# LayerNorm's scale and shift of the plain x and its residual addition as one VectorE step in the second MLP segment

## The chip, the cores and the metric

The kernel runs on one core of one Trainium2 chip (trn2), in one launch. The metric is the device time of that launch in microseconds. A difference of about 0.2% (3.3 us here) is what a measurement of this kernel can tell from no change.

## The reference, cut to what matters

Two encoder layers over 512 tokens of 1024 channels, all in float32. In each layer a token sublayer (attention, retention, gates) gives `y`, and then:

```python
def layer_norm(x, g, b):
    mu = jnp.mean(xf, axis=-1, keepdims=True)
    var = jnp.mean(jnp.square(xf - mu), axis=-1, keepdims=True)
    y = (xf - mu) * lax.rsqrt(var + LN_EPS) * g + b
...
    x = layer_norm(DEEPNORM_ALPHA * x + y, ln1_g[i], ln1_b[i])
    ffn = conv_glu_ffn(x, w_up[i], conv_w[i], conv_b[i], w_down[i])
    ple = jax.nn.sigmoid(x @ w_ple_gate[i]) * (p[i] @ w_ple_proj[i])
    x = layer_norm(DEEPNORM_ALPHA * x + ffn + ple, ln2_g[i], ln2_b[i])
```

The change touches the term `DEEPNORM_ALPHA * x` of the last line: where the normalised x gets its factor and shift, and where it is added to the sum.

## The kernel before, in words

**Matrix products.** float32 operands are split in two float32r parts, `hi` (a cast on ScalarE) and `lo` (the remainder, a subtraction on VectorE), and each product is three matmuls (`hi*hi`, `hi*lo`, `lo*hi`). Weights come as 128x1024 pieces from `in_wpack`. Many products are done in Strassen's manner, with seven instead of eight block products (`a c t1 t2 d t3 t4`), for which sums of weight blocks are made by transfers that add: a POOL-queue transfer adds a second block to `rawa` or `rawt`. In the same way `s`, `sh`, `sl` are sums of blocks of the activations and their two parts.

**Stages of a layer's second half.** `project()` makes x before the norm in four tiles `xn[0..3]` (128 tokens x 1024), and `normed` subtracts the mean and multiplies by 1/std there. `done1` turns `xn` by TensorE into `x1t`, the transposed operand, and applies the norm's factor g and shift b there per partition. `xn` itself, the plain x, is needed once more, for the residual, and gets its g and b (both times ALPHA, which ScalarE puts in on loading: tiles `lnh`) in `affine(t)`: for each half of 512 columns a multiplication and an addition on VectorE, `xn<-xn,lnh`, 16 instructions for the four tiles.

Then comes `pg()`, which runs the list `PG[l]`: the gate product of the embedding (`a c t1 t2 d t3 t4`), with the first of three MLP segments woven in (`0a` to `1t4` and `g`: blocks of the up-projection; `S`: sums; `T2`: second half of `done1`; `A0` to `A3`: `affine`). Then `down(0)`, `up_part(1)`, `down(1)`, `up_part(2)`, and the last down-projection. `R[0..3]` are four tiles that start as the embedding's projection; `ple_gate` multiplies them by the sigmoid of the gate (`R<-R,psg`), x is added, and each segment's down-projection adds its products out of PSUM (`into`: `R<-R,u`, `R<-R,v`).

**Adding x to R.** `RES_DMA = (0, 1)`: for tiles 0 and 1, once both halves of the gate are multiplied in, `residual()` issues a transfer on the POOL queue that adds `xn[t]` to `R[t]` (`R<-xn`, 512 KB). For tiles 2 and 3 `ple_gate` does it on VectorE, a half at a time (`R<-R,xn`).

**Buffers.** `xn`, `R`, the operands of the down-projection (`a`, `k`, `ss`, `sh`, `sl`), `gg`, `uh`, and part of the `hi`, `lo` and `raw` tiles all come out of one pool, `unit`, of 30 buffers of 128x1024 float32 (`N_UNIT = 30`). A buffer is reused once its last reader has finished. `lnh` has a pool of its own, with four buffers.

**Order.** TensorE's order is that of the program text. From the middle of each layer's first product to the end of `region()` the order on the other four engines, and which buffer a tile takes, is set when the kernel is built, by a planner (`_jobs`, `_dues`, `_best`, `_order`): it gives each instruction a due time from the TensorE work that needs it, walks through the engines with priced instructions and limited buffers, and keeps the best of 120 rounds of a random search started from `SEED`. An instruction under `prog.lazy = prog.pin = True`, as in `affine`, is due no later than the TensorE work that it stands behind in the text. On the chip every engine runs its instructions in that order, and waits for each one's inputs and buffer.

All instructions are issued through one helper, so the profile shows them under one line (L270); tiles tell them apart.

Of the kernel before, what the change touches and what calls it, by code (L numbers as in the profile page):

```python
# [12 lines left out]
ALU = mybir.AluOpType  # L13
# [43 lines left out]

TABLES_AT = ('0t4', '1t4')

PG = (tuple('a 0a T2 c S g S S S g 0c 1a A0 t1 A1 t2 A2 0t1 A3 1c 0t2 0d 0t3 1t1 0t4 d g 1t2 1d 1t3 t3 1t4 g t4'.split()),  # L60
        tuple('a 0a T2 S c S 0c 1a g g S 1c A0 t1 A1 0t1 A2 S 0t2 A3 t2 0d 0t3 1t1 0t4 1t2 1d 1t3 d 1t4 g t3 g t4'.split()))
PG_EARLY = "a"
RES_DMA = (0, 1)
A_DEEP = (4, 5, 5)
BOUND = ("p0", "t4a", "tr", "t4b", "p1")
VG_DEEP = 3
VG_PLAN = ("ga2", "0a")
VG_EARLY = "d"
S_SEQ = ("t1", "d", "t2", "t3")
UP_ORDER = ((tuple('0a 0t1 0c g g 0t2 0d 1a 0t3 g 0t4 g 1t1 1c 1t2 1d 1t3 s 1t4 s s s'.split()), tuple('0a 0t1 0c g g 0t2 0d 0t3 g 0t4 1a 1t1 1c 1t2 1d 1t3 s g s 1t4 s s'.split())),  # L70
            (tuple('0a 0t1 0c g g 0t2 0d 1a 0t3 g 0t4 g 1t1 1c 1t2 1d 1t3 s 1t4 s s s'.split()), tuple('0a 0t1 0c g g 0t2 0d 0t3 g 0t4 1a 1t1 1c 1t2 1d 1t3 s g s 1t4 s s'.split())))

DOWN = ("a", "c", "t1", "t2", "d", "t3", "t4")
CAP = {"unit.u": 30, "xt.xt": 1, "raw.raw": 3, "wsplit.hi": 3, "wsplit.lo": 3, "tmp.t": 6, "conv.cw": 2, "bias.B": 4, "psum.b": 8}
# [7 lines left out]
SET = {1: dict(soon=5, hold=6, reserve=10, load=16, work=25, scale=1.0, spare=2, near=10, seed=0, shake=0.0), 2: dict(soon=5, hold=6, reserve=10, load=16, work=25, scale=1.0, spare=2, near=10, seed=0, shake=0.0)}  # L82
ROUNDS = 120
WALK = 12
SEED = 3


VG_HELD = (('0t1', '1t1', '0t2', '0c', '1t2', '1a', '1d', '1t3'), ('0a', '0c', '0t1', '1t1', '1t3', '1t2', '0t3', '0t2', '1d'))
# [2 lines left out]
def _up_order(l, s):  # L91

    return UP_ORDER[l][s - 1] if s else PG[l]


def _up_blocks(l, s):

    t0 = 2 * sum(SEGS[:s])
    return [t0 + 2 * b for b in range(sum(k[0].isdigit() and k.endswith("t4") for k in _up_order(l, s)))]
# [386 lines left out]
def _best(jobs, rounds=None):  # L486

    import random
    rnd = random.Random(SEED)
    rounds = rounds or ROUNDS  # L490
# [289 lines left out]
def trunk(tc, wpack, x_nat, x_tr, head, p_tr, rpb, decay, ln_par, ln_col, conv, cos_t, sin_t, dist, xi_d, zd, ident_d, out):  # L780
    prog = Program(tc)
    nc = _Engines(prog)
# [3 lines left out]
    with ExitStack() as es:  # L786
# [22 lines left out]
        def unit_f(s, shape=(P, 1024)):  # L809
            return up.tile(list(shape), F32, tag="u", name=nm(s))  # L810

        def tmp(s, n=512):
            return tp.tile([P, n], F32, tag="t", name=nm(s))
# [480 lines left out]
        for i in range(2):  # L1294
            c = slice(i * 512, (i + 1) * 512)
# [114 lines left out]
        for l in range(DEPTH):  # L1410
# [380 lines left out]
            xn, xgb = [], []  # L1791
# [223 lines left out]
            def affine(t):  # L2015

                prog.lazy = prog.pin = True
                for h in range(2):
                    z = xn[t][:, h * 512:(h + 1) * 512]
                    nc.vector.tensor_mul(z, z, g1[h])  # L2020
                    nc.vector.tensor_add(z, z, b1[h])
                prog.lazy = prog.pin = False

            def project():
# [81 lines left out]
            R = [unit_f("R") for _ in range(4)]  # L2106
# [35 lines left out]
            def ple_gate(t, c, src, scale):  # L2142
                sg = tmp("psg")
                nc.scalar.activation(sg, src, AF.Sigmoid, scale=scale)
                nc.vector.tensor_mul(R[t][:, c], R[t][:, c], sg)
                if t not in RES_DMA:
                    nc.vector.tensor_add(R[t][:, c], R[t][:, c], xn[t][:, c])
                    return
                done[t] = done.get(t, 0) + 1
                if done[t] == 2:  # L2150
                    late.append(t)

            done, late = {}, []

            def residual():

                while late:
                    t = late.pop(0)
                    nc.gpsimd.dma_start(R[t], xn[t], accum_op=ALU.add)

            wx = {}

# [92 lines left out]
            def up_part(s):  # L2255

                t, state, st, n, S = 2 * sum(SEGS[:s]), {}, {}, 0, {}
                nb = len(_up_blocks(l, s))
                for k in _up_order(l, s):
                    if k in "gs":  # L2260
                        j = 2 * nb + n // 2
                        n += 1
                        up_half(j, t + j, state)
                    else:
                        b = int(k[0])
                        block(b, k[1:], t + 2 * b, st.setdefault(b, {}), None, S)
# [40 lines left out]
            def pg():  # L2307
                S, sg = {}, vg_sums(xf_at(xf))
                two = lambda name: [bank(name) for _ in range(2)]
                keep, u, v, state, blocks, n = {}, None, None, {}, {}, 0  # L2310
                nb = len(_up_blocks(l, 0))
                for key in PG[l]:
                    residual()
                    if key[0] in "TA":
                        (done1 if key[0] == "T" else affine)(int(key[1]))
                        continue
                    if key == "S":
                        r = next(sg)
                        if isinstance(r, dict):
                            S.update(r)  # L2320
                        continue
                    if key == "g":
                        j = 2 * nb + n // 2
                        n += 1
                        up_half(j, j, state)
                        continue
                    if key[0].isdigit():
                        b = int(key[0])
                        block(b, key[1:], 2 * b, blocks.setdefault(b, {}), xt, S)
                        continue  # L2330
                    def product(ps, first):
                        lh = {"a": lambda k, s, i: xt[:, k, s, i * P:(i + 1) * P],
                              "c": lambda k, s, i: xt[:, 4 + k, s, i * P:(i + 1) * P],
                              "t4": lambda k, s, i: xt[:, 4 + k, s, 256 + i * P:256 + (i + 1) * P]}.get(key)
                        if lh is None:
                            lh = lambda k, s, i: S[key][s][:, k, i * P:(i + 1) * P]
                        for j in range(2):
                            hi, lo = ws.get()
                            for i in range(2):
                                for kk in range(2):  # L2340
                                    k, r = 2 * j + kk, slice(kk * 512, (kk + 1) * 512)
                                    mm3(ps[i], lh(k, 0, i), lh(k, 1, i), hi[:, r], lo[:, r], first and k == 0, k == 3, not first)

                    if key in S_SEQ:
                        sums_out(key, S)
                    if key == "a":
                        u = two("u")
                        product(u, True)
                        keep["p1"] = [tmp("p1") for _ in range(2)]
                        for i in range(2):  # L2350
                            nc.scalar.copy(keep["p1"][i], u[i])
                    elif key == "c":
                        w = two("w")
                        product(w, True)
                        for i, t in enumerate(keep["p1"]):
                            nc.vector.tensor_add(t, t, w[i])
                        for i, t in enumerate(keep["p1"]):
                            ple_gate(i, N1, t, 1.0)
                    elif key == "t1":
                        v = two("v")  # L2360
                        product(v, True)
                        p5 = unit_f("p5", (P, 2, 512))
                        for i in range(2):
                            nc.scalar.copy(p5[:, i], v[i])
                    elif key == "t2":
                        product(u, False)
                        keep["u2"] = [tmp("u2") for _ in range(2)]
                        for i in range(2):
                            nc.scalar.copy(keep["u2"][i], u[i])
                    elif key == "d":  # L2370
                        product(v, False)
                        for i, t in enumerate(keep["u2"]):
                            nc.vector.tensor_add(t, t, v[i])
                        for i, t in enumerate(keep["u2"]):
                            ple_gate(i, N2, t, -1.0)
                    elif key == "t3":
                        product(u, False)
                        for i in range(2):
                            nc.vector.tensor_add(p5[:, i], p5[:, i], u[i])
                        for i in range(2):  # L2380
                            ple_gate(2 + i, N2, p5[:, i], -1.0)
                    else:
                        product(u, False)
                        for i in range(2):
                            ple_gate(2 + i, N1, u[i], 1.0)

            pg()
            st = [sp.tile([P, 2, 6], F32, tag="bn", name=nm("bn")) for _ in range(4)]
            residual()
            two = lambda name: [bank(name) for _ in range(2)]  # L2390
            def region():

# [12 lines left out]
            for s in (len(SEGS) - 1,):  # L2405
# [180 lines left out]
                t4 = products("t4", x4, s == 0)  # L2586
# [160 lines left out]
```

## Time and profile before

| | |
|---|---|
| median of 3 runs | 1650.58 us (1649.71 to 1650.64) |
| profiled execution, its own time | 1654.58 us |
| its span from first to last instruction | 1652.8 us |
| TensorE matmuls busy | 1632.7 us, 99% of the span |
| VectorE busy | 1331.4 us, 81% |
| ScalarE busy | 1011.9 us, 61% |
| mean granted TensorE clock | 0.995 |
| `pg()` and `down(0)` of layer 0 | about 447 to 585 us of the span |
| `pg()` and `down(0)` of layer 1 | about 1267 to 1400 us |
| `up_part(1)` of layer 1 | 1400 to 1484 us |

The span is what the trace shows; 1.78 us of the profiled execution lie around it. The profiled execution is 4.0 us above the median of the runs. Times in rows are microseconds from the span's start unless marked ns. In a row of the timeline the bracket gives the engine's idle time before the instruction and what ended it. TensorE's idle time and the stretches in which its clock was granted at half are the two things that can be won here without taking work away from it.

### The profile page before, as it was taken

Reading aid. Unit: us, or ns where it says so; the run is one execution under the profiler, and the core shown is the slowest. Engines: PE = TensorE matmul, PEld = TensorE weight load, DVE = VectorE, ACT = ScalarE, POOL = GpSimd, SP = SyncE. Lnnn points to the kernel's source line nnn. Section 1 sums busy time; section 2 is a strip of 40 time slices with the busy share of each in tenths; the row PEclk is TensorE's granted clock in tenths of the full one; section 3 lists DMA queues with packets and bytes.
Section 4 is the critical chain, followed back from the end, with each engine's and each line's share of the span. In section 5 each row is a group of like instructions: output and inputs, shape, how many; then the busy total and the mean of one; then the engine's idle time right before and its main releaser. Section 6 shows DMA issues by size and latency. Waiting matters only on the chain. (4 is left out here: it accounts for less than half of the span.)

```text
span 1652.8 us, 25767 instructions
## 1 busy us (share of the span) xinstructions
PE 1632.7 (99%) x9717; PEld 1454.2 (88%) x9717; DVE 1331.4 (81%) x2057; ACT 1011.9 (61%) x1522; POOL 267.4 (16%) x320
## 2 busy tenths in 40 slices
PE   9999999999999999999999999999999999999997
PEld 7889999888888898898888899998888987988986
DVE  6657998689997968768885779986799889687688
ACT  6656769654667656456484558795457574563554
POOL 1210212001211121111012112210012111111113
PEclk9999999999999999999999999999999999999999
DMA  8996768969899799888599867787588997988874
GB/s 306 270 244 148 181 154 201 283 204 251 194 296 260 193 257 223 230 259 208 171 263 252 254 166 189 192 227 242 196 252 223 317 238 203 250 198 264 236 178 116
DMA packets 111852, 371.53 MB, mean 225 GB/s; under 512 B 13168, under 2 KB 15728, under 8 KB 111728
## 3 DMA queue, kind: packets, MB, share of 16 engines
q0 software_dynamic: 39888, 143.15, 44.4%
q1 hardware_dynamic: 71840, 226.74, 38.3%
q8 instruction: 76, 1.25, 0.3%
q14 instruction: 48, 0.39, 0.1%
HBM read 336.28 MB, written 27.79 MB: 220 GB/s over the span
## 5 line engine op out<-in xcount | busy, mean ns | idle before, releaser
L270 DVE TENSOR_TENSOR lo<-rawa,hi 128x1024 fp32r<-128x1024 f32 (+1 forms) x214 | 255.9, 1202 | 74.2 <-ACT hi L270 66.9
L270 POOL DMA_DIRECT2D rawa<-in_wpack x162 | 143.4, 905 | 969.5 <-DVE lo L270 681.5
L270 ACT CAST hi<-rawa 128x1024 fp32r<-128x1024 f32 (+1 forms) x214 | 218.8, 1033 | 104.9 <-DMA rawa<-in_wpack 64.2
L270 DVE TENSOR_TENSOR lo<-raw,hi 128x1024 fp32r<-128x1024 f32 (+1 forms) x175 | 211.0, 1209 | 21.4 <-ACT hi L270 18.4
L270 PE MATMUL gt<-x1t,hi 128*128 128x512 f32 x640 | 197.5, 390 | 0.0
L270 ACT CAST hi<-raw 128x1024 fp32r<-128x1024 f32 (+1 forms) x151 | 156.4, 1039 | 38.6 <-PE u L270 17.1
L270 PEld LDWEIGHTS gt<-x1t,hi 128*128 128x128 f32 x640 | 118.8, 188 | 23.6
L270 PE MATMUL gt<-x1t,lo 128*128 128x512 f32 x320 | 124.5, 389 | 0.0
L270 PE MATMUL v<-lo,sh 128*128 128x512 f32 x216 | 84.2, 390 | 0.0
L270 PE MATMUL v<-hi,sh 128*128 128x512 f32 x216 | 84.1, 389 | 0.0
L270 PE MATMUL v<-hi,sl 128*128 128x512 f32 x216 | 84.0, 389 | 0.0
L270 PE MATMUL u<-sh,hi 128*128 128x256 f32 x288 | 81.9, 285 | 0.0
L270 PE MATMUL v<-sh,hi 128*128 128x256 f32 x288 | 81.7, 284 | 0.0
L270 PE MATMUL u<-xt,hi 128*128 128x256 f32 x448 | 81.5, 283 | 0.0
L270 PE MATMUL v<-sh,lo 128*128 128x256 f32 x288 | 81.5, 283 | 0.0
L270 PE MATMUL v<-sl,hi 128*128 128x256 f32 x288 | 81.5, 283 | 0.0
L270 PE MATMUL u<-sh,lo 128*128 128x256 f32 x288 | 81.5, 283 | 0.0
L270 PE MATMUL u<-sl,hi 128*128 128x256 f32 x288 | 81.5, 283 | 0.0
L270 ACT ACTIVATE uh<-u 128x512 f32<-128x512 f32 x60 | 35.8, 596 | 74.4 <-PE u L270 70.3
L270 PE MATMUL u<-hi,sl 128*128 128x512 f32 x200 | 78.7, 394 | 2.6 <-DVE sl L270 2.6
L270 PE MATMUL u<-lo,sh 128*128 128x512 f32 x200 | 78.5, 393 | 1.2 <-DVE lo L270 1.2
L270 PE MATMUL gt<-ybt,hi 128*128 128x512 f32 x256 | 79.5, 392 | 0.0
(310 smaller groups left out, 4791.4 us busy)
## 6 DMA issues: line engine op xcount, KB each, us to landing
raw<-in_wpack SPq DMA_DIRECT2D x171, 512.0 KB, 7.7
rawa<-in_wpack POOLq DMA_DIRECT2D x156, 512.0 KB, 7.4
rawa<-in_wpack SPq DMA_DIRECT2D x52, 512.0 KB, 7.0
rawt<-in_wpack SPq DMA_DIRECT2D x52, 512.0 KB, 7.2
rawt<-in_wpack POOLq DMA_DIRECT2D x52, 512.0 KB, 9.6
hi<-in_wpack POOLq DMA_DIRECT2D x40, 512.0 KB, 7.3
sx<-s_scr SPq DMA_DIRECT2D x32, 512.0 KB, 10.5
lo<-in_wpack POOLq DMA_DIRECT2D x16, 512.0 KB, 8.3
```

The costliest lines, as they stand in the source:

```text
L270: r = o.call(*[real(x) for x in o.a], **{k: real(v) for k, v in o.k.items()})
```

## The change

`affine(t)` gets a third instruction for each half: it adds the finished half of `xn[t]` to `R[t]` on VectorE. Its four calls leave `PG` for the list of the second MLP segment, `up_part(1)`, behind that segment's first two block products. The transfers `R<-xn` and the additions in `ple_gate` are removed, for all four tiles. The planner's search starts from another seed. TensorE's instructions and their order stay as they are; the planned order of the other engines is searched anew.

```diff
-PG = (tuple('a 0a T2 c S g S S S g 0c 1a A0 t1 A1 t2 A2 0t1 A3 1c 0t2 0d 0t3 1t1 0t4 d g 1t2 1d 1t3 t3 1t4 g t4'.split()),
-        tuple('a 0a T2 S c S 0c 1a g g S 1c A0 t1 A1 0t1 A2 S 0t2 A3 t2 0d 0t3 1t1 0t4 1t2 1d 1t3 d 1t4 g t3 g t4'.split()))
+PG = (tuple('a 0a T2 c S g S S S g 0c 1a t1 t2 0t1 1c 0t2 0d 0t3 1t1 0t4 d g 1t2 1d 1t3 t3 1t4 g t4'.split()),
+        tuple('a 0a T2 S c S 0c 1a g g S 1c t1 0t1 S 0t2 t2 0d 0t3 1t1 0t4 1t2 1d 1t3 d 1t4 g t3 g t4'.split()))
-RES_DMA = (0, 1)
 UP_ORDER: the second segment's list, in both layers
-  '0a 0t1 0c g g 0t2 0d 1a 0t3 g 0t4 g 1t1 1c 1t2 1d 1t3 s 1t4 s s s'
+  '0a 0t1 A0 0c A1 g A2 g A3 0t2 0d 1a 0t3 g 0t4 g 1t1 1c 1t2 1d 1t3 s 1t4 s s s'
-SEED = 3
+SEED = 1
 def affine(t):
     prog.lazy = prog.pin = True
     for h in range(2):
-        z = xn[t][:, h * 512:(h + 1) * 512]
+        c = slice(h * 512, (h + 1) * 512)
+        z = xn[t][:, c]
         nc.vector.tensor_mul(z, z, g1[h])
         nc.vector.tensor_add(z, z, b1[h])
+        nc.vector.tensor_add(R[t][:, c], R[t][:, c], z)
     prog.lazy = prog.pin = False
 def ple_gate(t, c, src, scale):
     nc.vector.tensor_mul(R[t][:, c], R[t][:, c], sg)
-    if t not in RES_DMA:
-        nc.vector.tensor_add(R[t][:, c], R[t][:, c], xn[t][:, c])
-        return
-    done[t] = done.get(t, 0) + 1
-    if done[t] == 2:
-        late.append(t)
-done, late = {}, []
-def residual():
-    while late:
-        t = late.pop(0)
-        nc.gpsimd.dma_start(R[t], xn[t], accum_op=ALU.add)
 def up_part(s):
     for k in _up_order(l, s):
-        if k in "gs":
+        if k[0] == "A":
+            affine(int(k[1]))
+        elif k in "gs":
 ...
 def pg():
     for key in PG[l]:
-        residual()
 ...
 pg()
-residual()
```

More of the change, by code (lines that the diff above doesn't have):

```diff
@@ L69 @@
 S_SEQ = ("t1", "d", "t2", "t3")
-UP_ORDER = ((tuple('0a 0t1 0c g g 0t2 0d 1a 0t3 g 0t4 g 1t1 1c 1t2 1d 1t3 s 1t4 s s s'.split()), tuple('0a 0t1 0c g g 0t2 0d 0t3 g 0t4 1a 1t1 1c 1t2 1d 1t3 s g s 1t4 s s'.split())),
-            (tuple('0a 0t1 0c g g 0t2 0d 1a 0t3 g 0t4 g 1t1 1c 1t2 1d 1t3 s 1t4 s s s'.split()), tuple('0a 0t1 0c g g 0t2 0d 0t3 g 0t4 1a 1t1 1c 1t2 1d 1t3 s g s 1t4 s s'.split())))
+UP_ORDER = ((tuple('0a 0t1 A0 0c A1 g A2 g A3 0t2 0d 1a 0t3 g 0t4 g 1t1 1c 1t2 1d 1t3 s 1t4 s s s'.split()), tuple('0a 0t1 0c g g 0t2 0d 0t3 g 0t4 1a 1t1 1c 1t2 1d 1t3 s g s 1t4 s s'.split())),
+            (tuple('0a 0t1 A0 0c A1 g A2 g A3 0t2 0d 1a 0t3 g 0t4 g 1t1 1c 1t2 1d 1t3 s 1t4 s s s'.split()), tuple('0a 0t1 0c g g 0t2 0d 0t3 g 0t4 1a 1t1 1c 1t2 1d 1t3 s g s 1t4 s s'.split())))
 DOWN = ("a", "c", "t1", "t2", "d", "t3", "t4")
```

## The prediction

> **What bounds the kernel now.** I read the page's head first, then TensorE's waits, then its timeline where it waits, then the timeline of the engine waited for, and last the chain.
>
> ```profile
> span 1652.8 us, 25767 instructions
> PE 1632.7 (99%) x9717; PEld 1454.2 (88%) x9717; DVE 1331.4 (81%) x2057; ACT 1011.9 (61%) x1522; POOL 267.4 (16%) x320
> ```
>
> TensorE's matmuls (PE) are busy for 99% of the span of 1652.8 us, and the change takes no matmul away. So all that can be won is TensorE's idle time and what its clock loses. Its waits, all of them that the view lists (waiting engine and tile, releaser: us, times, longest):
>
> ```profile
> PE u L270 <- DVE sl L270: 2.6, 1, 2.6
> PE w L270 <- DVE lo L270: 2.1, 1, 2.1
> PE w L270 <- ACT hi L270: 1.8, 1, 1.8
> PE u L270 <- DVE lo L270: 1.2, 1, 1.2
> PE warm L270 <- DVE warm L270: 1.2, 1, 1.2
> PE st L270 <- ACT kz L270: 0.7, 1, 0.7
> PE s L270 <- DVE qk L270: 0.6, 1, 0.6
> PE kz L270 <- DVE kf L270: 0.5, 1, 0.5
> PE u L270 <- DVE x1t L270: 0.4, 1, 0.4
> PE tr L270 <- DVE xn L270: 0.2, 1, 0.2
> ```
>
> Each of them occurs once. The first four are the largest; the timeline tells when they happen, and the windows view tells what the granted clock was after the largest:
>
> ```profile
> 482.43 0.50 PE L270 MATMUL u<-hi,sl 128*128 128x512 f32 x1 [2.59 <-DVE sl L270]
> 533.23 0.50 PE L270 MATMUL u<-lo,sh 128*128 128x512 f32 x1 [1.24 <-DVE lo L270]
> 1370.98 0.49 PE L270 MATMUL w<-hi,k 128*128 128x512 f32 x1 [1.82 <-ACT hi L270]
> 1373.59 0.80 PE L270 MATMUL w<-lo,k 128*128 128x512 f32 x1 [2.11 <-DVE lo L270]
> ```
>
> ```profile
> 483.91:487.32 3.41, 3.41 (x9) 2.67 (x8) 3.41 (x7) 0.00 (x0) 0.00 (x0) 0.50 1.04 233
> 1373.59:1378.20 4.61, 4.61 (x11) 3.64 (x12) 4.61 (x8) 4.24 (x5) 0.00 (x0) 0.50 0.60 125
> ```
>
> All four lie in the embedding's gate product and first MLP segment, where the change works: two in layer 0, two in layer 1. In a row of the windows the third number from the right, behind the five engines, is the clock: 0.50 for 3.41 us right after the gap of 2.59, and 0.50 for the 4.61 us after the last gap. At half clock half of that time is lost: 1.7 and 2.3 us. So this stage loses 2.59 + 1.24 + 1.82 + 2.11 = 7.76 us idle and 4.0 us by the clock, 11.8 us in all.
>
> Why VectorE was late each time:
>
> ```profile
> 477.00 0.69 DVE L270 TENSOR_TENSOR xn<-xn,lnh 128x512 f32<-128x512 f32 x1
> ...
> 478.74 1.29 DVE L270 TENSOR_TENSOR xn<-xn,lnh 128x512 f32<-128x512 f32 x2
> ...
> 481.08 0.69 DVE L270 TENSOR_TENSOR xn<-xn,lnh 128x512 f32<-128x512 f32 x1
> 481.68 1.29 DVE L270 TENSOR_TENSOR sl<-s,sh 128x512 fp32r<-128x512 f32 x2
> ...
> 530.14 0.76 DVE L270 TENSOR_TENSOR ss<-gg 128x256 f32<-128x256 f32 x2 [1.64 <-DMA R<-xn]
> ...
> 1354.92 0.75 DVE L270 SCALAR_TENSOR_TENSOR gg<-uh,cw,gg 128x511 f32<-128x511 f32 x1
> 1360.75 1.23 DVE L270 TENSOR_TENSOR lo<-rawa,hi 128x1024 fp32r<-128x1024 f32 x1 [5.08 <-DMA R<-xn]
> ```
>
> In layer 0 TensorE waits for `sl` at 481.68, and four instructions of `affine` stand just ahead of it. Later VectorE itself stands still for 1.64 us (layer 0) and 5.08 us (layer 1) until a transfer `R<-xn` has landed. Neither `ss<-gg` nor `lo<-rawa,hi` reads or writes R or xn. What ties them to the transfer is the pool: they are given the buffer that `xn` leaves, and that is free only when the transfer has read it. The chain of waits says the same for the program's end; its longest piece that isn't TensorE is
>
> ```profile
> 1349.67 10.95 DMA R<-xn
> ```
>
> **The change part by part.**
>
> *`affine` leaves this stage.* Its instructions, and the additions that stand there now:
>
> ```profile
> L270 DVE TENSOR_TENSOR xn<-xn,lnh x32: 681/696/711, 461.7 to 1308.6; 128x512 f32<-128x512 f32 x32
> L270 DVE TENSOR_TENSOR R<-R,xn x8: 683/689/699, 563.4 to 1395.5; 128x512 f32<-128x512 f32 x8
> L270 POOL DMA_DIRECT2D R<-xn x4: 867/867/874, 520.3 to 1349.7; - x4
>   DVE R L270: 13.6, 4
> ```
>
> Two of them in a row start 0.60 us apart (478.74 for 1.29 us holds two), so a layer's 16 take 9.6 us of VectorE out of this stage. Four ran just before `sl`: 4 x 0.60 = 2.4 us. Without them the gap of 2.59 us shrinks to 0.2, like the least in the list, and with it goes its half clock: -2.4 - 1.7 = -4.1.
>
> The *transfers go.* Then no buffer waits for them. Behind VectorE's 5.08 us lie the last two gaps (3.93 us) with their half clock (2.3), behind its 1.64 us the gap of 1.24: -7.5. POOL loses four issues of 0.87 us, and 13.6 us in which its queue stood until R was multiplied, with weight additions behind it. I cost that at nothing, since no row of TensorE's waits names a transfer; it can only help.
>
> *24 instructions enter the second segment* in each layer (16, the four additions of tiles 2 and 3, four new ones for tiles 0 and 1): 24 x 0.60 = 14.4 us of VectorE, beside
>
> ```profile
> 1400.30:1431.30 31.00, 31.00 (x217) 29.11 (x216) 15.87 (x17) 13.57 (x17) 5.48 (x7) 1.00 0.98 289
> ...
> 1458.00:1484.20 26.20, 26.20 (x134) 22.41 (x133) 25.29 (x43) 16.83 (x26) 5.30 (x7) 1.00 0.85 183
> sum 167.90, PE 167.90 PEld 151.66 DVE 123.06 ACT 99.30 POOL 31.04; mean PE 27.98 PEld 25.28 DVE 20.51 ACT 16.55 POOL 5.17
> ```
>
> The last row sums six windows that cover this segment in both layers (585 to 669 and 1400.3 to 1484.2): VectorE is idle for 167.90 - 123.06 = 44.8 us, and 28.8 come in. In layer 1 the first 31 us alone have 15.1 idle for 14.4. So I take 0. If the cover is gone, because they slide to the last window (0.9 us idle), up to 13.5 us of VectorE work stand ahead of that segment's operands; that end belongs to the slower side.
>
> *Loads of the constants* (`lnh`, four per layer on SP's queue, and four ScalarE scalings) can come later, into a stage with less traffic; they have a pool of their own: 0.
>
> *The new wait.* Each third instruction waits for the last product that the first segment adds to R:
>
> ```profile
> L270 DVE TENSOR_TENSOR R<-R,u x8: 680/683/700, 1376.2 to 1397.8; 128x512 f32<-128x512 f32 x8
> ```
>
> That is done by 1398.5, ahead of the segment's start at 1400, so the VectorE queue behind it (the segment's convolutions) isn't held. But until then all four `xn` keep their buffers: tiles 0 and 1, which now go by 1360.6 (1349.67 + 10.95), about 38 us longer. These are 2 of 30 buffers, in the very stretch where two instructions waited for such a buffer. The trace has no row for what will be short instead. Its bounds: below, a gain, since the order is searched anew and small gaps elsewhere in it (0.7 + 0.6 + 0.5 + 0.4 + 0.2 = 2.4 us) could close too; above, that the three gaps which hang on a buffer come back in full, 7.5 us. I take one gap of the middle size seen here with one window of half clock, 1.82 + 1.7 = 3.5, as nearest to what a shortage did in this stage.
>
> [...] Both stretches of half clock follow gaps of 1.8 to 2.6 us, so I let them go with the gaps. [...]
>
> Sum: -4.1 - 7.5 + 3.5 = -8.1 us. The profiled execution has 1654.58 (span 1652.8 and 1.78 around it), so 1646.5 for it; the median of the runs is 4.0 lower, and I let both fall by the same: 1650.58 - 8.1 = **1642.5**. If the profile's extra 4.0 us sit in just these waits, the gain in the timed runs is up to 4.0 smaller, 1646.5; without a new gap it is 1639.0. That is the likeliest case's own range.
>
> **The rivals.**
> 1. *Nothing takes the waits' place*: -4.1 - 7.5 = -11.6, 1639.0. For it: VectorE gets 9.6 us back in this stage. Against it: every planned stretch of this trace has some small gap.
> [...]
> 3. *Another buffer wait takes the transfers' place* with the same price in both layers: only `affine`'s share is won, -4.1, less small new gaps of up to 2.4 in the newly searched order: 1646.5 to 1648.9, about no change. For it: `ss` and `lo` waited for exactly such a buffer, and the change frees these later.
> 4. *Slower: a weight block's buffer comes free too late, so that its transfer is issued late and nothing covers it.* Price from the nearest rows: 10.95 us for such a transfer to land plus 1.23 for `lo`, and two windows of half clock, 3.4: 15.6 us for one. With the rest won, -11.6 + 15.6 = +4.0: 1654.6; it decides from new stalls of over 11.6 us upward, and is slower by more than 0.2% (3.3 us, about what can be told from no change) from 14.9. For it: 38 us more of two buffers. Against it: TensorE waited for no transfer in 1652 us.
>
> **How the numbers follow.** Chances: the forecast 0.48, rival 1 0.15, rival 2 0.05, rival 3 0.20, rival 4 0.12. The first three are faster, and a tenth of rival 3: 0.70; the rest of rival 3 is the same: 0.18; rival 4 slower: 0.12. The range reaches from 1637.5 (rival 1 and half of the small gaps closed) to 1653 (rival 3 and most of the way to rival 4), and leaves out about one in ten above and less below.
>
> **What would show it.** In the changed kernel's trace: no `R<-xn`; VectorE has no idle time ended by it; 16 `R<-R,xn` and 32 `xn<-xn,lnh`, all in or near the second segment; TensorE's waits on `sl` and on `lo` or `hi` in these stages gone, and no half clock there. [...] The prediction as a whole is wrong if the gaps in the newly searched order sum to more than the 11.6 us that go.

## The result, and the profile after

| | before | changed |
|---|---|---|
| median of 6 runs | 1652.29 us (1649.71 to 1655.04) | 1644.72 us (1644.16 to 1645.20) |
| ratio, 95% interval | | 0.9953 [0.9940, 0.9966] |
| profiled execution, its span | 1654.58 us, 1652.8 | 1644.46 us, 1642.7 |

The change makes the kernel 0.47% faster, 7.8 us [5.6, 9.9]. Forecast were 8.1 us and a median of 1642.5, which the measured one exceeds by 2.2. The page's head and all of TensorE's waits in the changed kernel (waiting engine and tile, releaser: us, times, longest):

```profile
span 1642.7 us, 25774 instructions
PE 1629.1 (99%) x9717; PEld 1451.7 (88%) x9717; DVE 1336.0 (81%) x2065; ACT 1017.4 (62%) x1525; POOL 267.4 (16%) x316
```

```profile
PE gt L269 <- DVE uh L269: 1.3, 1, 1.3
PE warm L269 <- DVE warm L269: 1.2, 1, 1.2
PE st L269 <- DVE kz L269: 0.5, 2, 0.4
PE o L269 <- DVE ta L269: 0.5, 1, 0.5
PE s L269 <- DVE qk L269: 0.3, 1, 0.3
PE tr L269 <- DVE xn L269: 0.3, 1, 0.3
PE w L269 <- DVE ta L269: 0.3, 1, 0.3
PE gt L269 <- DVE lo L269: 0.2, 1, 0.2
```

They sum to 4.6 us, the list of before to 11.3. All four of the large gaps are gone, and one of 1.3 us is new. The windows view, where before had half clock and over the two gate-product stages (third number from the right: the granted clock):

```profile
1371.37:1378.20 6.83, 6.83 (x32) 5.66 (x31) 6.83 (x10) 3.29 (x7) 1.73 (x2) 1.00 0.58 121
470.00:585.00 115.00, 114.79 (x675) 101.94 (x674) 97.40 (x135) 73.65 (x95) 16.60 (x19) 1.00 0.87 242
1266.00:1400.00 134.00, 133.70 (x781) 118.53 (x780) 119.56 (x165) 88.93 (x123) 21.33 (x25) 1.00 0.92 258
```

The clock is full throughout (1.00 in each row). 6.7 us less of waits and 4.0 us of half clock (half of 3.41 + 4.61 us at 0.50) make 10.7; the span of the profiled executions fell by 10.1. So the gain is where the prediction looked for it. The new gap stands where the moved instructions went (timelines of TensorE and VectorE, layer 0):

```profile
587.73 0.70 PE L269 MATMUL gt<-x1t,hi 128*128 128x512 f32 x2 [1.35 <-DVE uh L269]
```

```profile
580.96 2.49 DVE L269 TENSOR_TENSOR xn<-xn,lnh 128x512 f32<-128x512 f32 x4
583.36 1.28 DVE L269 TENSOR_TENSOR R<-R,xn 128x512 f32<-128x512 f32 x2
584.57 1.29 DVE L269 TENSOR_TENSOR xn<-xn,lnh 128x512 f32<-128x512 f32 x2
585.77 1.22 DVE L269 TENSOR_TENSOR lo<-raw,hi 128x1024 fp32r<-128x1024 f32 x1
586.91 0.68 DVE L269 TENSOR_TENSOR uh<-uh,w 128x512 f32<-128x512 f32 x1
```

Eight instructions of `affine` and a `lo` run ahead of the addition that reads TensorE's product `w` out of PSUM, and TensorE waits 1.35 us for that addition.

### The profile page after: what moved, and what is told of

The parts are those of the page before. It is cut to its first block, busy times and chain, and to the rows that moved or that the text cites. A ratio compares the mean times of both kernels' runs of the same rounds, so it can differ in the third digit from the quotient of the medians.

```text
span 1642.7 us, 25774 instructions
## 1 busy us (share of the span) xinstructions
PE 1629.1 (99%) x9717; PEld 1451.7 (88%) x9717; DVE 1336.0 (81%) x2065; ACT 1017.4 (62%) x1525; POOL 267.4 (16%) x316
## 5 line engine op out<-in xcount | busy, mean ns | idle before, releaser
L269 PE MATMUL u<-hi,sh 128*128 128x512 f32 x200 | 77.8, 389 | 0.0
```

The lines of the kernel that those rows point to most:

```text
L269: r = o.call(*[real(x) for x in o.a], **{k: real(v) for k, v in o.k.items()})
```

## The experiments

The first four ask which part carries the gain. My theory was that `affine` and the transfers did, by leaving the stage; the rival, that it was the order, searched anew.

**Only the seed, on the old kernel.**

```diff
-SEED = 3
+SEED = 1
```

> The kernel before with only the planner's seed changed from 3 to 1; nothing of the change itself. My theory (the gain is the affine instructions and the adding transfers leaving this stage): both stay, so the losses stay in kind: VectorE idle time ended by R<-xn is there again, and the time is within 4 us of the kernel before. Rival (the gain is the newly searched order): the time is 5 to 8 us below before, like the changed kernel.

Measured: 0.9947 [0.9935, 0.9960], 1644.75 us, 8.8 us below before and as fast as the changed kernel. My theory falls; the rival's mechanism came, with a little more than its 5 to 8 us. The transfers are still waited for, but by ScalarE (its waits), and TensorE's longest wait apart from the program's first stage (`warm`) is 0.8 us (its waits, the five largest):

```profile
ACT a L270 <- DMA R<-xn: 1.7, 1, 1.7
ACT hi L270 <- DMA R<-xn: 0.6, 1, 0.6
```

```profile
PE warm L270 <- DVE warm L270: 1.2, 1, 1.2
PE v L270 <- DVE sl L270: 1.2, 2, 0.8
PE s L270 <- DVE qk L270: 0.8, 2, 0.6
PE gt L270 <- DVE x1t L270: 0.8, 1, 0.8
PE v L270 <- DVE R L270: 0.3, 1, 0.3
```

**The change without its seed.**

```diff
-SEED = 1
+SEED = 3
```

> The changed kernel with the planner's seed left at 3. My theory: 5 to 10 us below before, no half clock in the two gate-product stages, no VectorE idle time ended by a transfer of x; against the changed kernel within 3 us. Rival (order): no gain that can be told, within 3 us of before.

Measured: 0.9955 [0.9942, 0.9967], 1645.91 us. That is 7.4 us below before, as my theory said, but it doesn't speak for that theory alone: the changed program's order was searched anew, from the same seed. So the structure without the seed also gives the whole gain. The two don't add: either one suffices.

**Transfers replaced in place, `affine` left where it was.**

```diff
 def residual():
-    nc.gpsimd.dma_start(R[t], xn[t], accum_op=ALU.add)
+    for c in (N1, N2):
+        nc.vector.tensor_add(R[t][:, c], R[t][:, c], xn[t][:, c])
```

> The kernel before with its two transfers R<-xn per layer replaced by VectorE additions at the same place of the text (four more VectorE instructions per layer in the gate-product stage); affine stays where it was, seed 3. My theory: the transfers' share of the gain comes alone, about 7.5 us less 0 to 2.4 for the added VectorE work where it is full: 4 to 7.5 us below before, and a wait on sl or lo behind affine's instructions remains. Rival (VectorE's load in this stage is what counts, not the transfers): no gain or up to 3 us slower, since the stage gets 2.4 us more of VectorE per layer. Rival (order): anything within 4 us of before.

Measured: 0.9960 [0.9947, 0.9974], 1646.43 us. 6.6 us fit my theory's range; the rival of VectorE's load is out, as the stage got 2.4 us per layer more of it and still won. But the theory's sign did not come: `affine` stayed, and yet TensorE's longest wait on `sl` is 0.7 us, where before had 2.6. The order was searched anew here too, and the third reading fits that better.

**The transfer kept for two tiles, in the second segment.**

```diff
 def affine(t):
     for h in range(2):
-        nc.vector.tensor_add(R[t][:, c], R[t][:, c], z)
+        if t > 1:
+            nc.vector.tensor_add(R[t][:, c], R[t][:, c], z)
+    if t < 2:
+        nc.gpsimd.dma_start(R[t], xn[t], accum_op=ALU.add)
```

> The changed kernel, but tiles 0 and 1 of x are added by the transfer again, now behind affine in the second segment; tiles 2 and 3 on VectorE as in the changed kernel; seed 1. My theory (a transfer costs where a short buffer waits for its end): affine's share stays won, at least 4.1 us below before; if VectorE or another engine shows idle time ended by R<-xn in the second segment, up to 5 us of the changed kernel's gain are lost, and if no buffer is short there, the time is that of the changed kernel or up to 1.5 us less, since VectorE has four additions less where the changed kernel has its gap of 1.35 us. Rival (the transfer costs by its traffic, wherever it runs): the weight loads beside it land later and TensorE waits on them.

Measured: 0.9972 [0.9960, 0.9983], 1647.90 us: some 3 us of the changed kernel's gain are missing. No compute engine is idle until an `R<-xn`, so no buffer wait explains it, and my theory, which then allowed for no loss, missed. TensorE's longest waits are on `lo`, `sl` and `hi`. The longest of all, 1.55 us on `sl`, ends at 557.33 us, before the first of these transfers is issued at 570.52; so another order has at least a part in the loss. How much the traffic does is not settled.

**One order held fixed.** To part the terms from the search, the next three play back the order and choice of pools that the planner had found for the kernel before, and edit one thing in it. Their edits are given partly in words.

*The transfers release `xn`'s buffers* (they add another tile, from HBM, so the sum of tiles 0 and 1 lacks x):

```diff
-        order = _best(jobs)
+        order = held order of the kernel before
-    nc.gpsimd.dma_start(R[t], xn[t], accum_op=ALU.add)
+    nc.gpsimd.dma_start(R[t], rscr[l][t * P:(t + 1) * P, :], accum_op=ALU.add)
```

> The kernel before with its planned order and its choice of pools held fixed, instruction for instruction; only the four transfers onto R read the embedding's projection in HBM (r_scr) instead of xn, so x is left out of tiles 0 and 1 and another tile added. They issue at the same place and move the same 512 KB, but no longer hold xn's buffers. Theory (ss and lo waited for the buffer that the transfer was still reading): both VectorE waits of 1.64 and 5.08 us on R<-xn go without another wait in their place, TensorE's gaps of 1.24, 1.82 and 2.11 us and layer 1's half clock with them: 5 to 7.5 us below before. Rival (the transfer's traffic or its share of the POOL queue made the weights late): VectorE still waits there, no more than 2 us of gain.

Measured: 0.9959 [0.9947, 0.9972], 6.8 us [4.6, 8.8] of 1652.69. The buffer is the cause: transfers of the same size at the same place of the order no longer stop VectorE (1.64 and 5.08 us in before, no such wait here), though they take longer to land (median 9.5 us against 8.4). SP's queue, which issues weight loads and in before waits 10.5 us for `R<-xn`, has none to wait for either; the run doesn't part the two. Of TensorE's four large gaps only layer 0's first is left, and the small waits are those of before, which shows that the order was held (its three longest waits, and that gap in the timeline):

```profile
PE u L270 <- DVE sl L270: 2.8, 1, 2.8
PE warm L270 <- DVE warm L270: 1.2, 1, 1.2
PE st L270 <- ACT kz L270: 0.7, 1, 0.7
```

```profile
483.35 0.50 PE L270 MATMUL u<-hi,sl 128*128 128x512 f32 x1 [2.83 <-DVE sl L270]
```

*Four `affine` instructions one place later:*

```diff
+    late = the four xn instructions of tile 1, layer 0, ahead of sl
+    order = order without late, with late behind that sl
```

> The kernel before with its planned order held fixed, but for four affine instructions of layer 0 (tile 1) that stood between the other VectorE work before sl and now stand directly behind it. Theory (affine's place in the VectorE order made sl late): TensorE's gap of 2.59 us shrinks to 0.2 to 0.6 and the half clock behind it goes: 3 to 4.1 us below before; the layer 1 gaps stay as they are. Rival (sl's late start comes from the work before that): gap at least 1.5 us, gain under 1.5 us. [...]

Measured: 0.9994 [0.9983, 1.0005], where 3 to 4.1 us were expected. The gap on `sl` shrinks as expected, and 10 us later another one of 2.01 us stands, with 3.41 us of half clock (timelines of TensorE and VectorE, and the window):

```profile
480.75 0.50 PE L270 MATMUL u<-hi,sl 128*128 128x512 f32 x1 [0.42 <-DVE sl L270]
491.17 0.39 PE L270 MATMUL w<-x1t,lo 128*128 128x256 f32 x1 [2.01 <-DVE lo L270]
```

```profile
480.01 1.28 DVE L270 TENSOR_TENSOR sl<-s,sh 128x512 fp32r<-128x512 f32 x2
481.22 5.75 DVE L270 TENSOR_TENSOR xn<-xn,lnh 128x512 f32<-128x512 f32 x9
...
489.89 1.22 DVE L270 TENSOR_TENSOR lo<-raw,hi 128x1024 fp32r<-128x1024 f32 x1
```

```profile
491.80:495.21 3.41, 3.41 (x18) 3.41 (x18) 3.41 (x4) 0.00 (x0) 1.26 (x2) 0.50 0.95 324
```

The four joined the rest of `affine`, now nine in a row, and `lo` behind them became the late one. Putting work off by a few places, while VectorE was full, moved the gap.

*Both edits:*

```diff
+    the transfers' other source, and the four xn instructions behind sl
```

> Both of the last two edits on the held order of before. Theory: the terms add, 8 to 11.6 us below before, 1642 to 1645 us, no half clock before the program's end. This is what removing the waits is worth with nothing else searched anew. Rival: a later wait takes over what the first set free, so that the sum is at least 3 us less than the two alone.

Measured: 0.9950 [0.9935, 0.9964], 8.3 us, within the range of 8 to 11.6, but not to be told from the first edit alone. Layer 1 is clear, layer 0 has the moved gap (2.03 us, and a clock of 0.50 from 492.05 to 495.46). That is the rival's mechanism; that the sum is 3 us less than the two alone isn't so, since the second alone gave nothing that can be told.

**More seeds**, to see the spread that a search brings. The edits are the seeds alone.

```diff
-SEED = 3
+SEED = 2
```

> The kernel before with the planner's seed 2, since seed 1 alone gave the whole gain and my theory that the change's own removals carry it has fallen. New theory (what was lost belongs to the one order that seed 3 found): 1643 to 1647.5 us, no half clock or at most one. Rival (affine and transfers in this stage are slower for most orders, seed 1 was lucky): 1648 to 1655 us, with waits on sl behind affine or on a buffer that a transfer holds.

```diff
-SEED = 1
+SEED = 2
```

> The changed kernel with the planner's seed 2. Theory (the change itself is worth 0 to 2 us beside the spread of the orders): 1643 to 1648 us, overlapping with the old kernel's seeds 1, 2 and 4. Rival (the change gives a real gain over the old structure): 1643.5 to 1646 while the old structure's seeds lie at 1647 or more but for seed 1.

```diff
-SEED = 3
+SEED = 4
```

> The kernel before with the planner's seed 4. Theory (the loss belongs to the one order of seed 3): 1643 to 1647.5 us. Rival (the old structure is slower for most orders): 1648 to 1655 us.

```diff
-SEED = 1
+SEED = 4
```

> The changed kernel with the planner's seed 4. Theory: 1643 to 1648 us, as the old structure's seeds 1, 2 and 4. Rival: below all of these but seed 1, at 1643.5 to 1646.

Ratios to the kernel before (the old structure with seed 3):

| seed | old structure | changed structure |
|---|---|---|
| 1 | 0.9947 [0.9935, 0.9960], 1644.75 us | 0.9953 [0.9940, 0.9966], 1644.72 us |
| 2 | 0.9971 [0.9960, 0.9983], 1648.00 us | 0.9984 [0.9974, 0.9995], 1648.72 us |
| 3 | 1 | 0.9955 [0.9942, 0.9967], 1645.91 us |
| 4 | 0.9981 [0.9972, 0.9990], 1649.17 us | 0.9957 [0.9944, 0.9969], 1644.82 us |

The old structure's mean is 0.9975, the changed one's 0.9962. Seed by seed the difference is +0.0006, +0.0013, -0.0045, -0.0024: mean -0.0013 (2 us) with a scatter of 0.0026, which four pairs don't tell from nothing. No one theory fits all: seeds 2 and 4 of the old structure lie 3 to 5 us above seed 1, where the rival expected them, and seed 2 of the changed one is as slow.

The traces add what the times don't tell: where `affine` stands, TensorE often waits behind it. In the old structure the longest such wait is 2.6 us with seed 3, 1.9 with seed 2 and 2.8 with seed 4, always in the gate-product stage on an `sl` or `lo` that stands behind `affine`; with seed 1 TensorE has no wait over 0.8 there. In the changed structure it is 1.3 to 1.4 us in all four, always in the second segment, behind the instructions that moved there. Seed 4 of the old structure (VectorE, then TensorE):

```profile
1298.10 3.09 DVE L270 TENSOR_TENSOR xn<-xn,lnh 128x512 f32<-128x512 f32 x5
...
1302.84 1.28 DVE L270 TENSOR_TENSOR xn<-xn,lnh 128x512 f32<-128x512 f32 x2
1304.05 2.35 DVE L270 TENSOR_TENSOR lo<-rawa,hi 128x1024 fp32r<-128x1024 f32 x2
```

```profile
1305.31 0.58 PE L270 MATMUL u<-sh,lo 128*128 128x256 f32 x1 [2.76 <-DVE lo L270]
```

With seeds 1, 2 and 4 of the old structure ScalarE waits up to 1.8 us for a transfer `R<-xn`, and TensorE has no gap in the 20 us after that. So a place for `affine` with smaller gaps may be a gain of the change itself; as every order differs in more than that, the eight kernels suggest it and don't show it.

**`affine` spread over the second segment**, seed 1:

```diff
-'0a 0t1 A0 0c A1 g A2 g A3 0t2 0d 1a 0t3 g 0t4 g 1t1 ...'
+'0a 0t1 0c A0 g g A1 0t2 0d A2 1a 0t3 g A3 0t4 g 1t1 ...'
```

> The changed kernel with the four calls of affine spread over the second segment's list (one between each two to four block products instead of all behind the second), seed 1. Theory (the new gap of 1.35 us in layer 0 comes from 24 VectorE instructions packed into 20 us ahead of what empties a PSUM bank): that gap goes, 1643 to 1644.5 us, a little under the changed kernel. Rival (xn's buffers, now held longer still, run short in the second segment): waits for buffers there, 1646 to 1650 us. Rival (order): 1643 to 1648 us with gaps elsewhere, nothing told about the place.

Measured: 0.9946 [0.9934, 0.9959], 1643.21 us (1642.79 to 1643.58), the fastest kernel here; its interval overlaps the changed kernel's. In the changed kernel's list only `A0` stands right behind the second block product, the others behind the third and the two `g` after it; here they stand further apart. The gap of 1.35 us is gone, as the first theory says (TensorE's waits, the longest three):

```profile
PE warm L269 <- DVE warm L269: 1.2, 1, 1.2
PE st L269 <- DVE kz L269: 0.8, 2, 0.7
PE u L269 <- DVE x1t L269: 0.8, 1, 0.8
```

Its order was searched anew too, and TensorE's waits in it sum to 4.9 us, against 4.6 in the changed kernel. So the missing gap alone doesn't account for the 1.5 us; what does remains open.

## Why the prediction was right, and where its reasons were not

**What bounds the kernel: right.** The four gaps and the half clock behind them were most of what could be won, and all of them went.

**The transfers, -7.5: right in size and mechanism, on this order.** With the order held, freeing the buffers alone is worth 6.8 us [4.6, 8.8]. What I did not see is that this is a property of the order: seed 1 keeps the transfers, has ScalarE wait for the transfers instead, and no large gap of TensorE follows.

**`affine`, -4.1: not shown as a gain of its own.** "Without them the gap of 2.59 us shrinks to 0.2" holds nearly (0.42), but when the four were put off by a few places, the next `lo` took over the gap, 2.01 us with its half clock, and nothing was won. I did not ask what is late next. `affine` taken out of the stage with the order held was not tried, so its -4.1 stays open; that the stage can hold `affine` without such a gap, seed 1 of the old structure and the run with the transfers replaced in place show.

**The 24 instructions, 0: gaps of 1.35 and 0.2 us stand behind them in layer 0.** I compared their sum with VectorE's idle time over 31 us of the segment. They ran within 22 us (567.9 to 590.0), and TensorE waited for the PSUM reader that stood behind eight of them.

**The new buffer wait, 3.5: it did not come.** In the two gate-product stages TensorE is idle for 0.2 and 0.3 us in all. With the gaps behind the 24 in its place, the sum is -11.6 + 1.55 = -10.05, and the profiled span fell by 10.1: by mechanism rival 1, whose sum was -11.6, came nearer than the forecast.

**The new search, up to 2.4: far too small.** From seed to seed the same structure moves by up to 8.8 us (1644.75 to 1653.5). I listed the seed among the edits and priced it by the small gaps of one order. It is the largest term: the seed alone gives the whole gain, and so does the structure alone. The losses went because they belonged largely to the one order of the kernel before, which either edit replaces; "the change removes what costs" is not shown as the reason for "the cost goes".

**Profile against median: luck.** I let both fall by the same 8.1. The profiled execution fell by 10.1, the median by 7.6 (1652.29 to 1644.72), because the profiled execution of before lay 2.3 us above its median. That the measured 7.8 lies so near to 8.1 comes of this and of the 3.5 us for a wait that did not come: two errors that nearly cancel. The time of 1642.5 also rested on a median of three runs, 1650.58, which six runs put at 1652.29. The 52 runs of the kernel before that stand beside these experiments span 1649.06 to 1655.47 us, and their mean falls with the granted clock: 1653.75 us at 0.996 (21 runs), 1651.54 at 0.997 (24 runs). By the granted 0.50, one half-clock stretch of 3.41 us takes 0.001 of the mean clock and 1.7 us. So the profiled execution's extra 4.0 us are of the size of two to three such stretches; that some runs have more of them than others is my estimate from the granted clocks, 0.995 to 0.998 in the 52 runs. The changed kernel's profile has no half clock before 1636.90 us, 2.7 us after TensorE's last matmul; its runs have clocks of 0.998 and 0.999 and lie within 1.04 us.

**Rival 2, the half clock isn't the gaps' doing: wrong here.** With the gaps the half clock went: the two stretches at 0.50 of before (3.41 and 6.83 us) have no like in the changed kernel, whose rows of both stages show 1.00. Of the 14 profiles, four have a half clock before TensorE's work ends: before, both held orders with the moved instructions, and seed 4 of the old structure. There it comes with gaps of 1.82 to 2.76 us; the profiled executions of the other ten have mean clocks of 0.998 and 0.999 (last section).

## What to carry to other kernels

Where a planner or scheduler is run again, compare several of its draws on both sides before an edit is credited: here four seeds of one structure spread over 9 us (old) and 4 us (changed), where the edit seemed to win 8. To test a mechanism, hold the order fixed and take away one wait; that showed the buffer's cost cleanly, and showed that moving late work back by a few instructions only moves the gap. When work is moved into an engine's idle time, look for the instruction right behind it that TensorE waits for, not only at the sum of the idle time.

## What the runs showed of the hardware

A gap needn't be long for the half clock, and its length alone doesn't tell whether one comes. TensorE's gaps, and the granted clock that the windows view shows with them:

| kernel | gap, us | ends at | clock |
|---|---|---|---|
| before | 2.59 | 482.43 | 0.50 for 3.41 us from 483.91 |
| before | 1.82 | 1370.98 | 0.50 for 6.83 us from 1371.37; the gap of 2.11 lies in it |
| held order, `affine` put off | 2.01 | 491.17 | 0.50 for 3.41 us from 491.80 |
| the same, layer 1 | 2.0 | | 0.50 for 6.83 us from 1372.44 |
| held order, both edits | 2.03 | 490.54 | 0.50 for 3.41 us from 492.05 |
| old structure, seed 4 | 2.76 | 1305.31 | 0.50 for 6.82 us from 1304.64, before the gap's end |
| held order, no buffer wait | 2.83 | 483.35 | 1.00 from 478.13 to 488.36 |
| old structure, seed 2 | 1.9 | | mean of the profiled execution 0.998 |

The rows of the two longest gaps, 2.76 with half clock and 2.83 without:

```profile
1304.64:1311.46 6.82, 6.15 (x26) 5.86 (x26) 6.82 (x10) 1.26 (x3) 1.73 (x2) 0.50 1.06 241
```

```profile
478.13:481.54 3.41, 2.39 (x11) 1.66 (x9) 3.41 (x5) 1.68 (x3) 0.86 (x1) 1.00 0.95 315
481.54:484.95 3.41, 1.60 (x7) 1.34 (x8) 3.41 (x6) 2.60 (x4) 0.86 (x1) 1.00 0.93 185
484.95:488.36 3.41, 3.41 (x17) 2.83 (x16) 3.41 (x7) 0.59 (x1) 0.00 (x0) 1.00 1.01 227
```

What else decides isn't shown: no run sets a gap's length or place by itself.

What the half clock costs can be read off matmuls of one shape. In the first stretch of before they start 0.43 us apart, behind it 0.23 us:

```profile
483.94 0.63 PE L270 MATMUL u<-hi,sl 128*128 128x512 f32 x1
484.37 0.63 PE L270 MATMUL u<-hi,sh 128*128 128x512 f32 x1
...
487.57 0.39 PE L270 MATMUL u<-hi,sl 128*128 128x512 f32 x1
487.80 0.39 PE L270 MATMUL u<-hi,sh 128*128 128x512 f32 x1
```

By these starts a stretch of 3.41 us loses about 1.6 us, an estimate; by the granted 0.50 it was 1.7.
